# Decoder block on one core: the work between the output projection and the Strassen units in another order

## The chip, the core and the metric

One core of one Trainium2 chip runs the whole block in one launch. Its engines are TensorE (PE; its weight loads are listed as PEld), VectorE (DVE), ScalarE (ACT), GpSimd (POOL) and SyncE (SP, which only issues DMAs here); each runs its own queue in order and waits for others by semaphores. The metric is the device time of an execution in microseconds (us), lower is better. A time is the median of several executions; the profile is one execution more, with a time of its own.

## What is computed

x is 512 tokens by 1024 features in float32. After a mixer stage (gated linear attention, GLA, and sparse attention, NSA) the block ends with

```python
mixed = sigmoid(merge_gla) * (o_gla @ w_proj_gla) + sigmoid(merge_nsa) * (o_nsa @ w_proj_nsa)
x = x + rms_norm(mixed @ w_out, norm_mix_post)
h = rms_norm(x, norm_ffn_pre)
f = (silu(h @ w_ffn_gate) * (h @ w_ffn_up)) @ w_ffn_down     # 1024 -> 2816 -> 1024
x = x + rms_norm(f, norm_ffn_post)
```

and, in GLA, the gates are `log_sigmoid(a_lr @ w_alpha2 + b_alpha)`, whose running sums are taken per head.

## The kernel before

Features lie on the 128 partitions, tokens on the free axis (512 columns), so a matrix product is made of row blocks of 128 output features. Float32 accuracy comes from three products: each operand is split into a high part (a cast to fp32r on ACT) and a low part (the difference), and PE adds high by high, high by low and low by high. A low part is made in one of two ways: one subtraction on DVE, or a negated copy on ACT to which an accumulating DMA, issued by POOL, adds the source ("on_dma"). `Stream` (lines 32 to 75) loads weight tiles (128x1024, 512 KB) through SP one ahead and splits them; `st.on_dma` (line 172) names the tiles whose low part goes by DMA.

The stretch of the change goes so (lines 880 to 1233). The output projection has 8 row blocks; blocks 3 to 7 are made by token halves (`out_half(n, e)`, e = 0, 1 for tokens 0 to 255 and 256 to 511), first all first halves, then the second halves. Their squares are summed on POOL; `out_sums(e)` sums them over the partitions with matmuls by ones (`token_sums`) and takes the power -1/2 (`rsqrt_mean`: DVE, then POOL). `resid(e)` spreads that scale with matmuls (`over_partitions`, line 221, the "scale product"), and makes for each of 8 row blocks: x1 = out * scale + x (two DVE operations), h2h (ACT) and h2l (DVE). `resid_squares(e)` squares x1 on ACT and sums on POOL; `norm2(e)` makes from these the scale of the feed-forward norm, `normed(e)` the normed input on DVE.

The feed-forward layer has 22 row blocks. The first three ("plain" blocks, `NPLAIN`) work on the unnormed h2 and are scaled when evacuated (`plain_out`): blocks 0 and 1 by halves (`ffn_half(e, w, ps)`, gate and up weights of a block, 8 rows of k, 12 matmuls in all for a row of both blocks), block 2 in whole (`third`). The other 19 are made by Strassen-Winograd units (`unit(n)`, from N0 = 3 on): a 2x2 split of weights and inputs, gate and up products together in 7 products of 12 matmuls of 256 columns. The weights' sums s1, s2 (`prep_s`) and s3, s4 (`prep_t`) are made on DVE and split by `split_pair`; the inputs' forms b11, t2, t3, t1, b21, t4, b22 by `x_forms`. The products of a unit share two PSUM banks, and each has its evacuation before the next product into its bank.

The order on an engine is set when the program is built: a planner walks the instructions in the order in which they are written, and with its own cost estimates gives each engine the earliest written one that it takes to be ready. So a written order is a priority; `tc.issue_after(ins)` adds a fixed place behind an instruction of the same engine. A tile with a tag waits for the release of the tile that had its buffer. Before, the second residual's scale product stands behind row k = 2 of plain block 1's first half (`marks[2]`, line 1191).

The tail makes the last row block of the down projection by halves, too (lines 1272 to 1299): `tail_out(e)` multiplies by the scale, adds x1 and stores; for the second half every third add is on POOL.

Of the kernel before, what the change touches and what calls it, by code (L numbers as in the profile page):

```python
# [16 lines left out]
S = 512  # L17
# [74 lines left out]
def hybrid_block_kernel(ctx: ExitStack, tc: tile.TileContext, I, outT):  # L92
# [79 lines left out]
    st.on_dma = set(with_att) | {(x, n) for x in "gu" for n in range(1, NPLAIN)}  # L172
# [30 lines left out]
    def token_sums(acc, tag, blocks=range(NT)):  # L203

        ps = bank(tag)
        for i in blocks:
            for a in range(len(acc)):
                pe.matmul(ps[:, i:i + 1], acc[a][:, i * 128:(i + 1) * 128], ones[:, 0:1],  # L208
                          start=(a == 0), stop=(a == len(acc) - 1))
        return ps  # L210
# [127 lines left out]
    def gates_gla():  # L338
# [12 lines left out]
        for h in range(HG):  # L351
            pool.tensor_tensor(out=lam[:, h], in0=lows[h], in1=lam[:, h], op=OP.subtract)
# [555 lines left out]
    sq2 = quads("sq2_", 4, F32, "e")  # L908
# [57 lines left out]
    def resid(e, after=None):  # L966
        t = halves[e]
        rb = over_partitions(rs1, "tp", blocks[e], after)
        for k in range(KD):
# [6 lines left out]
            dve.scalar_tensor_tensor(out=lo, in0=y, scalar=g_fpre[:, k:k + 1], in1=hi.bitcast(F32),  # L976
                                     op0=OP.mult, op1=OP.subtract)
        return last

    def resid_squares(e):  # L980
        t = halves[e]
        for k in range(KD):
            act.activation(out=sq2[k // 2][:, k % 2, t], in_=x1[k][:, t], func=AF.Square)
            if k > 0:
                pool.tensor_tensor(out=sq2[0][:, 0, t], in0=sq2[0][:, 0, t], in1=sq2[k // 2][:, k % 2, t], op=OP.add)
# [3 lines left out]
    def norm2(e, after):  # L989
        r = slice(2 * e, 2 * e + 2)  # L990
        ps = token_sums([sq2[0][:, 0, :]], "tp", blocks[e])
        rsqrt_mean(rs2[:, r], ps[:, r], D, EPS)
        ps = over_partitions(rs2, "tp", blocks[e], after)
        act.copy(rb_x[:, halves[e]], ps[:, halves[e]])

    def ffn_half(e, w, ps):
# [3 lines left out]
        for k in range(KD):  # L1000
# [77 lines left out]
    sums = {}  # L1078

    def prep_s(n):  # L1080
        t = flat(ffn.tile([128, 2, S], F32, tag="sa", bufs=2, name="s12"))
        g, u = raws[n, "w_gate"], raws[n, "w_up"]
        dve.tensor_tensor(out=t[:, 0:512], in0=u[:, 0:512], in1=u[:, 512:1024], op=OP.add)
        dve.tensor_tensor(out=t[:, 512:1024], in0=t[:, 0:512], in1=g[:, 0:512], op=OP.subtract)
        sums[n] = t
        split_pair(n, t, ("s1", "s2"))

    def prep_t(n):
        t = flat(ffn.tile([128, 2, S], F32, tag="sa", bufs=2, name="s34"))
        g, u = raws.pop((n, "w_gate")), raws.pop((n, "w_up"))  # L1090
        dve.tensor_tensor(out=t[:, 0:512], in0=g[:, 0:512], in1=u[:, 0:512], op=OP.subtract)
        dve.tensor_tensor(out=t[:, 512:1024], in0=g[:, 512:1024], in1=sums.pop(n)[:, 512:1024], op=OP.subtract)
        split_pair(n, t, ("s3", "s4"))
# [8 lines left out]
    def x_form(name, segs):  # L1102

        his, los = [], []
        for src, hi, lo in segs:
            split(hi, lo, src)
# [3 lines left out]
        XF[name] = (his, los)  # L1110

    def x_forms():
        def at(i):
            return flat(hT[:, 2 * i:2 * i + 2, :]), flat(hTl[:, 2 * i:2 * i + 2, :])

        def bfull(t):
            return t.rearrange("p q t -> p (q t)")

        b11, b12, b21, b22 = [bfull(x) for x in (nb[0][0], nb[0][1], nb[1][0], nb[1][1])]
# [3 lines left out]
        t2 = [slot(4), slot(5)]  # L1123
        for i in range(2):
# [254 lines left out]
```

## Time and profile before

| | us |
|---|---|
| three executions: median (lowest to highest) | 920.99 (920.01 to 922.46) |
| the profiled execution: time | 921.21 |
| its span, first to last instruction | 919.4 |
| PE busy in it | 883.9 |
| DVE / ACT / POOL busy | 541.6 / 464.1 / 126.2 |
| mean granted TensorE clock | 0.987 |

The span is what the trace shows; the time has 1.8 us around it. A timeline row gives start, duration, engine, line of the kernel and operation, and in brackets how long the engine had been idle and what ended that. A granted clock of 1.00 is 2.4 GHz, 0.50 is 1.2 GHz. A row of PE is one matmul from its start to its modelled end, so rows overlap.

### The profile page before, as it was taken

To read this page: it belongs to the slowest core of one execution; us is meant where nothing else is said; L and a number is where in the kernel's file an instruction comes from. 1 tells how busy PE (TensorE), PEld (TensorE's weight loads), DVE (VectorE), ACT (ScalarE), POOL (GpSimd) and SP (SyncE) were. 2 spreads that over 40 slices of the span, in tenths; PEclk is the share of its full clock that TensorE was granted. 3 is DMA by queue.
4 is the path that set the end of the run, shared out by engine and by line. 5 is a ranking of instruction groups with operands and counts; after the bars stand their busy time and mean duration, and the time that the engine had idled before them with its cause. 6 is when DMAs were issued, how large, how long until landed. Compare 5 with 4: busy or idle time off the path is not lost. (4 is left out here: it accounts for less than half of the span.)

```text
span 919.4 us, 13174 instructions
## 1 busy us (share of the span) xinstructions
PE 883.9 (96%) x5074; PEld 762.0 (83%) x5074; DVE 541.6 (59%) x1008; ACT 464.1 (50%) x830; POOL 126.2 (14%) x156
## 2 busy tenths in 40 slices
PE   9999899999999999999999989799999999999995
PEld 8897677887788777777888977799999999788884
DVE  8214744443463998877675277986777778422224
ACT  6335324333442888887545447665665556323220
POOL 1100512010110000010001344021121110001011
PEclk9999899999999999999999999899999999999997
DMA  6232221312242254354237547397777772533312
GB/s 233 83 111 92 69 72 66 91 48 91 71 149 64 68 116 114 92 115 104 58 113 258 160 127 192 83 241 160 170 171 187 185 157 58 172 83 106 84 61 93
DMA packets 36480, 109.64 MB, mean 119 GB/s; under 512 B 4188, under 2 KB 6252, under 8 KB 36288
## 3 DMA queue, kind: packets, MB, share of 16 engines
q1 hardware_dynamic: 26944, 81.44, 28.6%
q0 software_dynamic: 8752, 26.80, 15.5%
q8 instruction: 40, 0.66, 0.3%
q10 hardware_dynamic: 720, 0.54, 0.2%
q14 instruction: 24, 0.20, 0.1%
HBM read 94.61 MB, written 4.19 MB: 107 GB/s over the span
## 5 line engine op out<-in xcount | busy, mean ns | idle before, releaser
L58 ACT CAST whi<-wraw 128x1024 fp32r<-128x1024 f32 (+3 forms) x98 | 96.1, 981 | 217.2 <-PE ps_mm L184 125.1
L64 DVE TENSOR_TENSOR wlo<-wraw,whi 128x1024 fp32r<-128x1024 f32 (+3 forms) x82 | 92.8, 1133 | 118.5 <-ACT whi L58 118.0
L183 PE MATMUL ps_mm<-hT_hi,whi 128*128 128x512 f32 x376 | 153.6, 408 | 2.2 <-DVE gq L296 2.2
L185 PE MATMUL ps_mm<-hT_hi,wlo 128*128 128x512 f32 x376 | 151.1, 402 | 1.3 <-DVE wlo L64 0.7
L184 PE MATMUL ps_mm<-hT_lo,whi 128*128 128x512 f32 x376 | 149.7, 398 | 0.0
L185 PEld LDWEIGHTS ps_mm<-hT_hi,wlo 128*128 128x128 f32 x376 | 71.4, 190 | 19.0 <-DVE wlo L64 1.5
L183 PEld LDWEIGHTS ps_mm<-hT_hi,whi 128*128 128x128 f32 x376 | 71.6, 190 | 17.8 <-ACT dd L370 2.6
L184 PEld LDWEIGHTS ps_mm<-hT_lo,whi 128*128 128x128 f32 x376 | 71.6, 190 | 14.9
L744 ACT ACTIVATE p<-p,mx 128x512 f32<-128x512 f32 (+1 forms) x64 | 35.9, 561 | 5.8 <-DVE mx L742 5.4
L201 DVE TENSOR_TENSOR pl<-ps_tp,ph 128x512 fp32r<-128x512 f32 (+1 forms) x64 | 31.0, 488 | 9.6 <-ACT ph L200 8.8
L62 POOL DMA_DIRECT2D wlo<-wraw x16 | 13.9, 867 | 164.5 <-ACT wlo L61 135.7
L1056 POOL DMA_DIRECT2D w_uu<-in_w_up x19 | 16.5, 867 | 145.4 <-ACT w_uu L1055 131.8
L934 POOL TENSOR_TENSOR acc<-acc,nsq 128x512 f32<-128x512 f32 x8 | 10.3, 1287 | 184.6 <-ACT nsq L933 184.6
L742 DVE CUSTOM_DVE_ANT_0 p<-ps_sc,causal 128x512 f32<-128x512 f32 (+1 forms) x64 | 29.9, 485 | 6.2 <-PE ps_sc L735 5.7
L200 ACT CAST ph<-ps_tp 128x512 fp32r<-128x512 f32 (+1 forms) x64 | 26.7, 416 | 5.8 <-PE ps_tp L784 4.1
L784 PE MATMUL ps_tp<-ident,p 128*128 128x128 f32 x160 | 27.7, 273 | 0.0
L784 PEld LDWEIGHTS ps_tp<-ident,p 128*128 128x128 f32 x160 | 20.5, 140 | 6.6
L183 PE MATMUL ps_mm<-gla_hi,whi 128*128 128x512 f32 x64 | 25.9, 405 | 0.0
L184 PE MATMUL ps_mm<-gla_lo,whi 128*128 128x512 f32 x64 | 25.4, 397 | 0.0
L185 PE MATMUL ps_mm<-gla_hi,wlo 128*128 128x512 f32 x64 | 25.4, 397 | 0.0
L1072 ACT CAST w_d0h<-s 128x1024 fp32r<-128x1024 f32 x13 | 13.6, 1047 | 23.3 <-PE ps_acc L1148 9.8
L1072 ACT CAST w_hl<-s 128x1024 fp32r<-128x1024 f32 x12 | 12.5, 1044 | 24.4 <-PE ps_tp L1148 8.7
(934 smaller groups left out, 2556.8 us busy)
## 6 DMA issues: line engine op xcount, KB each, us to landing
wraw<-in_w_t SPq DMA_DIRECT2D x40, 512.0 KB, 3.5
wraw<-in_w_gate SPq DMA_DIRECT2D x21, 512.0 KB, 5.3
rw<-in_w_up SPq DMA_DIRECT2D x19, 512.0 KB, 3.8
wlo<-wraw POOLq DMA_DIRECT2D x16, 512.0 KB, 4.5
wraw<-in_w_down SPq DMA_DIRECT2D x16, 512.0 KB, 3.6
wlo<-in_w_gate POOLq DMA_DIRECT2D x13, 512.0 KB, 8.4
wraw<-in_w_tok SPq DMA_DIRECT2D x12, 440.0 KB, 4.1
w_uu<-in_w_up POOLq DMA_DIRECT2D x19, 256.0 KB, 6.9
```

Of the source, the lines that this page charges most:

```text
L58: self.nc.scalar.copy(hi[:, :cols], raw[:, :cols])
L64: self.nc.vector.tensor_tensor(out=lo[:, :cols], in0=raw[:, :cols], in1=hi[:, :cols].bitcast(F32), op=OP.subtract)
L183: pe.matmul(ps[:, t], wh[:, c], xh(k)[:, t], start=(k == 0), stop=False)
L184: pe.matmul(ps[:, t], wh[:, c], xl(k)[:, t], start=False, stop=False)
L185: marks.append(pe.matmul(ps[:, t], wl[:, c], xh(k)[:, t], start=False, stop=(k == ktot - 1)))
L200: act.copy(hi, src)
L201: dve.tensor_tensor(out=lo, in0=src, in1=hi.bitcast(F32), op=OP.subtract)
L742: dve.tensor_tensor_reduce(out=o, in0=s, in1=causal[:, S - n:S], scale=-1.0, scalar=-NEG, op0=OP.add, op1=OP.min, accum_out=mx[:, i:i + 1])
L744: act.activation(out=o, in_=o, func=AF.Exp, scale=-1.0, bias=mx[:, i:i + 1], accum_out=z[:, i:i + 1])
L784: pe.transpose(tp[:, i * 128:(i + 1) * 128], p[:, OFF[i] + k * 128:OFF[i] + (k + 1) * 128], ident)
L1056: pool.dma_start(lo, src, accum_op=OP.add)
L1072: act.copy(hi, t)
```

## The change

Ten edits, some of them small:

- The first unit's raw weights are loaded early, once more, into two buffers (`early`), and its sums s1..s4 are made ahead of the output projection's row blocks. s1, s2 are split by ACT and an accumulating DMA behind the first residual's last cast; s3, s4 by ACT and DVE behind `x_forms`.
- u0, the up weights of plain block 0, joins the tiles whose low part is made by DMA. The up weights of block 2 get buffers of their own.
- Plain block 0's first half is cut: rows 0 and 1, `out_sums(1)`, rows 2 to 4, the second residual (its scale product behind row 4, in place of row 2 of block 1), rows 5 to 7.
- The norms' sums and scales are placed apart (`norm2_sums`, `norm2_scale`), the second half's sums before the last two rows of block 1.
- Forms b11 and b21, which need the first half only, go ahead of `normed(1)`; t2 is one tile of 1024 columns.
- Plain block 0 is evacuated before the first unit, 1 after it, 2 after the second unit.
- Later units' sums s1..s4 are made in one go (`prep_st`), the first one's behind the last form.
- `token_sums` takes all blocks of its first input first.
- The four subtractions in `gates_gla` move from POOL to DVE.
- Tail: the first half's scale product stands behind four rows of the second third of the sum, not behind all eight; every second add of the second half is on POOL.

```diff
-    st.on_dma = set(with_att) | {(x, n) for x in "gu" for n in range(1, NPLAIN)}
+    st.on_dma = set(with_att) | {("u", 0)} | {(x, n) for x in "gu" for n in range(1, NPLAIN)}
...
-        for i in blocks:
-            for a in range(len(acc)):
+        for a in range(len(acc)):
+            for i in blocks:
...
-            pool.tensor_tensor(out=lam[:, h], in0=lows[h], in1=lam[:, h], op=OP.subtract)
+            dve.tensor_tensor(out=lam[:, h], in0=lows[h], in1=lam[:, h], op=OP.subtract)
...
-    sq2 = quads("sq2_", 4, F32, "e")
+    early = [flat(quad("e%d" % i, F32, "early%d" % i)) for i in range(2)]
...
+    st.place["u", 2] = lambda: [flat(quad("e%d" % i, F32R, "u2_%d" % i)) for i in (2, 3)]
...
-    def split_pair(n, t, names):
+    def split_pair(n, t, names, after=None, on_dma=False):
         hi, lo = next_slot()
-        with tc.issue_after(h2_made.ins):
+        with tc.issue_after(after.ins) if after else nullcontext():
             act.copy(hi, t)
-        dve.tensor_tensor(out=lo, in0=t, in1=hi.bitcast(F32), op=OP.subtract)
+            if on_dma:
+                act.activation(out=lo, in_=t, func=AF.Copy, scale=-1.0)
+        if on_dma:
+            pool.dma_start(lo, t, accum_op=OP.add)
+        else:
+            dve.tensor_tensor(out=lo, in0=t, in1=hi.bitcast(F32), op=OP.subtract)
...
+    def prep_st(n, after=None):
         g, u = raws.pop((n, "w_gate")), raws.pop((n, "w_up"))
+        s12 = sums_s(g, u, after)
+        split_pair(n, s12, ("s1", "s2"))
+        split_pair(n, sums_t(g, u, s12), ("s3", "s4"))
...
-        x_form("b11", [(b11, *at(0))])
         dve.tensor_tensor(out=b11, in0=b12, in1=b11, op=OP.subtract)
...
-        x_form("b21", [(b21, flat(quad("e0", F32R, "x4h")), flat(quad("e1", F32R, "x4l")))])
...
+    for raw, x in zip(early, ("w_gate", "w_up")):
+        nc.sync.dma_start(raw, I[x][N0])
+    s12 = sums_s(*early)
+    s34 = sums_t(*early, s12)
     for n in BYHALF:
         out_half(n, 0)
-    for x in ("w_gate", "w_up"):
-        load(N0, x)
     out_half(3, 1)
     out_half(4, 1)
     out_sums(0)
+    for x in ("w_gate", "w_up"):
+        load(N0, x)
     out_half(5, 1)
-    resid(0)
+    on_act, on_dve = resid(0)
     for n in (6, 7):
         out_half(n, 1)
-    out_sums(1)
     resid_squares(0)
...
-    ffn_half(0, w0, first)
+    ffn_half(0, w0, first, range(0, 2))
+    out_sums(1)
+    marks = ffn_half(0, w0, first, range(2, 5))
+    resid(1, marks[-1])
+    ffn_half(0, w0, first, range(5, 8))
+    resid_squares(1)
+    split_pair(N0, s12, ("s1", "s2"), on_act, True)
...
-    marks = ffn_half(0, w1, second)
-    h2_made = resid(1, marks[2])
-    resid_squares(1)
-    marks = ffn_half(1, w0, first)
-    norm2(0, marks[5])
-    ffn_half(1, w1, second)
+    ffn_half(0, w1, second, range(0, 4))
+    norm2_sums(0)
+    ffn_half(0, w1, second, range(4, 8))
+    marks = ffn_half(1, w0, first, range(0, 2))
+    norm2_scale(0, marks[-1])
+    ffn_half(1, w0, first, range(2, 8))
...
     normed(0)
+    x_form("b11", [(b11, *at(0))])
+    ffn_half(1, w1, second, range(0, 6))
+    norm2_sums(1)
+    ffn_half(1, w1, second, range(6, 8))
...
+    marks = prod(third[0], w2, h2(h2h), h2(h2l), 0, 2, KD)
+    norm2_scale(1, marks[-1])
+    x_form("b21", [(b21, flat(quad("e0", F32R, "x4h")), flat(quad("e1", F32R, "x4l")))])
+    normed(1)
+    prod(third[0], [x[:, 256:1024] for x in w2], h2(h2h), h2(h2l), 2, 6, KD)
+    end = x_forms()
+    prep_g(N0)
+    prep_u(N0)
+    split_pair(N0, s34, ("s3", "s4"))
...
-    for n, (pg, pu) in enumerate((first, second, third)):
-        plain_out(n, pg, pu)
+    plain_out(0, *first)
...
         unit(n)
+        if n == N0:
+            plain_out(1, *second)
+        if n == N0 + 1:
+            plain_out(2, *third)
         if n + 1 < KF:
-            prep_s(n + 1)
-            prep_t(n + 1)
+            prep_st(n + 1, end)
...
-            eng = pool if e == 1 and k % 3 == 0 else dve
+            eng = pool if e == 1 and k % 2 == 0 else dve
...
-    down_half(1, (1,))
-    tail_out(0)
+    prod(psd, [x[:, 0:512] for x in wd[1]], fh, fl, 8, 4, KF, halves[1])
+    rb = over_partitions(rs3, "tp", blocks[0])
+    prod(psd, [x[:, 512:1024] for x in wd[1]], fh, fl, 12, 4, KF, halves[1])
+    tail_out(0, rb)
```

## Rows read from the trace of the kernel before

**Rows 1.** The page's line of the engines: busy time in us (share of the span), x instructions.
```profile
PE 883.9 (96%) x5074; PEld 762.0 (83%) x5074; DVE 541.6 (59%) x1008; ACT 464.1 (50%) x830; POOL 126.2 (14%) x156
```

**Rows 2.** Busy time of the engines in stretches: from:to, its length, then for PE, PEld, DVE, ACT and POOL the busy us (x instructions), the granted TensorE clock, the DMA engines' share, GB/s.
```profile
520.18:561.00 40.82, 36.20 (x291) 34.48 (x291) 31.10 (x65) 23.86 (x51) 18.93 (x23) 1.00 0.43 126
...
574.31:590.88 16.57, 11.03 (x64) 9.78 (x62) 16.03 (x24) 10.77 (x15) 0.87 (x1) 0.79 0.37 66
...
590.88:606.00 15.12, 15.12 (x126) 14.97 (x127) 13.71 (x21) 9.84 (x15) 2.59 (x3) 1.00 0.66 166
```

**Rows 3.** PE's timeline around the change: start, us, engine, line, operation, what it writes and reads, [idle time before it and what ended that]. L221 is a scale product, ps_tp at 523.00 for the first residual and at 545.25 for the second; 528.40 and 528.75 begin the last two rows of row block 7's second half, three matmuls each; L1148 is a Strassen unit.
```profile
523.00 0.61 PE L221 MATMUL ps_tp<-ident,rs 128*128 128x128 f32 x4
...
528.40 0.28 PE L183 MATMUL ps_acc<-hT_hi,whi 128*128 128x256 f32 x1
...
528.75 0.28 PE L183 MATMUL ps_acc<-hT_hi,whi 128*128 128x256 f32 x1
...
545.25 0.61 PE L221 MATMUL ps_tp<-ident,rs 128*128 128x128 f32 x4
...
579.14 0.58 PE L1148 MATMUL ps_tp<-hT_hi,w_d0h 128*128 128x256 f32 x1 [3.26 <-ACT hT_hi L200]
...
584.61 0.38 PE L1148 MATMUL ps_tp<-hT_hi,w_d1h 128*128 128x256 f32 x1
...
590.88 0.39 PE L1148 MATMUL ps_tp<-x4h,whi 128*128 128x256 f32 x1 [1.68 <-DVE us L1157]
```

**Rows 4.** DVE's timeline, 520 to 557, same columns: first sums of the first unit (L1083, L1092), the first and the second residual's first product (L973), u0's low part (L64), the second residual's last operation (L976).
```profile
523.10 0.69 DVE L1083 TENSOR_TENSOR s<-rw 128x512 f32<-128x512 f32 x1 [2.58 <-DMA rw<-in_w_up]
...
525.47 0.74 DVE L973 TENSOR_TENSOR slot<-slot,ps_tp 128x256 f32<-128x256 f32 x2
...
536.15 1.23 DVE L1092 TENSOR_TENSOR s<-rw,s 128x512 f32<-128x512 f32 x1
...
537.30 1.76 DVE L64 TENSOR_TENSOR wlo<-wraw,whi 128x1024 fp32r<-128x1024 f32 x1
...
545.89 0.42 DVE L973 TENSOR_TENSOR slot<-slot,ps_tp 128x256 f32<-128x256 f32 x1 [6.44 <-PE ps_tp L221]
...
556.25 0.70 DVE L976 SCALAR_TENSOR_TENSOR h2l<-slot,vecs,h2h 128x256 fp32r<-128x256 f32 x1 [0.18 <-ACT h2h L975]
```

**Rows 5.** ACT's and POOL's timeline: the cast of u0's high part, and the issue of an accumulating DMA, of plain block 2's gate weights, behind ACT's negated copy.
```profile
534.81 1.03 ACT L58 CAST whi<-wraw 128x1024 fp32r<-128x1024 f32 x1
...
538.33 0.90 POOL L62 DMA_DIRECT2D w_d1l<-wraw  x1 [0.35 <-ACT w_d1l L61]
```

**Rows 6.** DMA issues by line: count, KB each, median us from issue to landing. The first from the page, the second from the same list for 525 to 575.
```profile
wlo<-wraw POOLq DMA_DIRECT2D x16, 512.0 KB, 4.5
...
w_g3l<-in_w_gate POOLq DMA_DIRECT2D x1, 512.0 KB, 11.0
```

**Rows 7.** DVE's timeline from the second residual's end to the first unit's own evacuations: normed inputs (L1099), a difference among the forms (L1122), two low parts (L201), a plain evacuation (L1028), the unit's first evacuation (L1157).
```profile
556.87 3.73 DVE L1099 SCALAR_TENSOR_TENSOR nb<-slot,vecs,rb_x 128x256 f32<-128x256 f32 x8
...
571.16 3.25 DVE L1099 SCALAR_TENSOR_TENSOR nb<-slot,vecs,rb_x 128x256 f32<-128x256 f32 x8
...
574.33 1.22 DVE L1122 TENSOR_TENSOR nb<-nb,nb 128x1024 f32<-128x1024 f32 x1
...
580.33 2.35 DVE L201 TENSOR_TENSOR hT_lo<-nb,hT_hi 128x1024 fp32r<-128x1024 f32 x2
...
584.41 0.68 DVE L1028 TENSOR_TENSOR fa<-ps_sc,rb_x 128x512 f32<-128x512 f32 x1
...
590.41 0.41 DVE L1157 TENSOR_TENSOR us<-ps_tp,us 128x256 f32<-128x256 f32 x1
```

**Rows 8.** Timelines of POOL, DVE and PE in the GLA stage: the four subtractions of the gates (L352), the scans (L357), an evacuation (L296), a difference (L367), and the PE row that waited for the evacuation with the first and the last of twelve slow ones behind it.
```profile
90.60 6.87 POOL L352 TENSOR_TENSOR lam<-low,lam 128x512 f32<-128x512 f32 x4 [60.82 <-ACT lam L350]
...
91.91 4.47 DVE L357 TENSOR_TENSOR_SCAN lam<-keep,lam 128x512 f32<-128x512 f32 x2 [3.37 <-POOL lam L352]
...
98.80 0.68 DVE L296 TENSOR_TENSOR gq<-ps_mm,rb_x 128x512 f32<-128x512 f32 x1
...
102.89 1.09 DVE L367 TENSOR_TENSOR dd<-lam 128x512 f32<-128x512 f32 x1 [1.88 <-POOL gku L390]
...
104.65 2.70 DVE L357 TENSOR_TENSOR_SCAN lam<-keep,lam 128x512 f32<-128x512 f32 x2
...
99.62 0.47 PE L183 MATMUL ps_mm<-hT_hi,whi 128*128 128x512 f32 x1 [2.18 <-DVE gq L296]
...
101.66 0.63 PE L183 MATMUL ps_mm<-hT_hi,whi 128*128 128x512 f32 x1
...
106.36 0.63 PE L185 MATMUL ps_mm<-hT_hi,wlo 128*128 128x512 f32 x1
```

**Rows 9.** Timelines of DVE and PE in the tail: the first half's first products (L1287) and adds (L1289), PE's scale product of the second half, a pair of adds while POOL adds, DVE's last add.
```profile
904.52 0.75 DVE L1287 TENSOR_TENSOR y<-y,ps_tp 128x256 f32<-128x256 f32 x2 [3.23 <-PE ps_tp L221]
...
905.19 0.75 DVE L1289 TENSOR_TENSOR y<-y,x1r 128x256 f32<-128x256 f32 x2
...
908.97 1.12 PE L221 MATMUL ps_tp<-ident,rs 128*128 128x128 f32 x4 [1.02 <-POOL rs L215]
...
911.71 0.84 DVE L1289 TENSOR_TENSOR y<-y,x1r 128x256 f32<-128x256 f32 x2
...
915.05 0.72 DVE L1289 TENSOR_TENSOR y<-y,x1r 128x256 f32<-128x256 f32 x1
```

More of the change, by code (lines that the diff above doesn't have):

```diff
@@ L975, in resid @@
             last = act.activation(out=hi, in_=y, func=AF.Copy, scale=g_fpre[:, k:k + 1])
-            dve.scalar_tensor_tensor(out=lo, in0=y, scalar=g_fpre[:, k:k + 1], in1=hi.bitcast(F32),
-                                     op0=OP.mult, op1=OP.subtract)
-        return last
+            end = dve.scalar_tensor_tensor(out=lo, in0=y, scalar=g_fpre[:, k:k + 1], in1=hi.bitcast(F32),
+                                           op0=OP.mult, op1=OP.subtract)
+        return last, end
     def resid_squares(e):
@@ L982, in resid_squares, with norm2_sums, norm2_scale, ffn_half @@
         for k in range(KD):
-            act.activation(out=sq2[k // 2][:, k % 2, t], in_=x1[k][:, t], func=AF.Square)
+            sq = sq2[0][:, t] if k == 0 else sq2[1 + (k - 1) % 6 // 2][:, halves[(k - 1) % 2]]
+            act.activation(out=sq, in_=x1[k][:, t], func=AF.Square)
             if k > 0:
-                pool.tensor_tensor(out=sq2[0][:, 0, t], in0=sq2[0][:, 0, t], in1=sq2[k // 2][:, k % 2, t], op=OP.add)
+                pool.tensor_tensor(out=sq2[0][:, t], in0=sq2[0][:, t], in1=sq, op=OP.add)
     rs2 = ffn.tile([128, NT], F32, name="rs2")
-    def norm2(e, after):
+    def norm2_sums(e):
         r = slice(2 * e, 2 * e + 2)
-        ps = token_sums([sq2[0][:, 0, :]], "tp", blocks[e])
+        ps = token_sums([sq2[0]], "tp", blocks[e])
         rsqrt_mean(rs2[:, r], ps[:, r], D, EPS)
+    def norm2_scale(e, after):
         ps = over_partitions(rs2, "tp", blocks[e], after)
         act.copy(rb_x[:, halves[e]], ps[:, halves[e]])
-    def ffn_half(e, w, ps):
+    def ffn_half(e, w, ps, ks=range(KD)):
         t = halves[e]
         marks = []
-        for k in range(KD):
+        for k in ks:
             i, j = k // 2, k % 2
@@ L1105, in x_form @@
         for src, hi, lo in segs:
-            split(hi, lo, src)
+            act.copy(hi, src)
+            last = dve.tensor_tensor(out=lo, in0=src, in1=hi.bitcast(F32), op=OP.subtract)
             n = hi.shape[1] // 256
@@ L1110, in x_form, with at @@
         XF[name] = (his, los)
+        return last
+    def at(i):
+        return flat(hT[:, 2 * i:2 * i + 2, :]), flat(hTl[:, 2 * i:2 * i + 2, :])
     def x_forms():
[L1113 to L1119, printed above, removed]
         seg = (slice(0, 512), slice(512, 1024))
-        x_form("b11", [(b11, *at(0))])
         dve.tensor_tensor(out=b11, in0=b12, in1=b11, op=OP.subtract)
-        t2 = [slot(4), slot(5)]
-        for i in range(2):
-            dve.tensor_tensor(out=t2[i], in0=b22[:, seg[i]], in1=b11[:, seg[i]], op=OP.subtract)
-        hi, lo = at(1)
-        x_form("t2", [(t2[i], hi[:, seg[i]], lo[:, seg[i]]) for i in range(2)])
+        t2 = flat(ffn.tile([128, 2, S], F32, tag="sa", bufs=2, name="t2"))
+        dve.tensor_tensor(out=t2, in0=b22, in1=b11, op=OP.subtract)
+        x_form("t2", [(t2, *at(1))])
         dve.tensor_tensor(out=b12, in0=b22, in1=b12, op=OP.subtract)
```

47 lines of the change are left out of this document (20 added, 27 removed).

## The prediction

> **What bounds the kernel now.** I read the page's engine line first: TensorE (PE) is busy 96% of the span [rows 1], so a change of order can only win PE's waits, its half-clock time, and what comes after its last product. The table of stretches [rows 2] shows where these lie near the change. From the first half of row block 5 to the last plain half (520.18 to 561.0) PE is busy 36.2 of 40.8 us; in the first Strassen units 11.0 of 16.6, at a mean granted clock of 0.79; after 590.88 it waits no more (15.12 of 15.12 us). Busy time flatters, since a matmul's row (0.28 us) is longer than the distance to the next one, so I count work: 256-column matmuls start every 0.117 us (three in the 0.35 from 528.40 to 528.75, [rows 3]), 512-column ones take twice that. At 590.88 PE had issued 62 matmuls of Strassen units (counted in its timeline); had they run without a gap up to there, the units would have begun at 590.88 - 62 x 0.117 = 583.6. I call this the zero point of the units, and price the middle of the change by how far it moves.
>
> Then the timelines of PE and of VectorE (DVE) side by side. PE waits 3.3 us at 579.14 for a ScalarE (ACT) cast that follows a DVE chain, runs some two dozen matmuls at half clock (to 584.61), and waits 1.7 us at 590.88 for a DVE evacuation [rows 3]. DVE runs almost without a break from 571.16 to 591 [rows 7]. So DVE's queue sets the zero point, and the question is when DVE begins it and how much stands in it.
>
> **The middle: the second half's scale.** The first half's residual starts on DVE at 525.47, though its scale left PE at 523.6: the first sums of the first Strassen unit (three operations from 523.10) stand before it, the fourth at 536.15 and the low part of the up weights of plain block 0 ("u0", 1.76 us at 537.30) inside it [rows 3, 4]. The change makes the sums before 520, when DVE is idle (its sources are loaded once more, 2 x 512 KB, for which the hiding work is the row blocks of the output projection; were they late by x, DVE would start x late), and gives u0's low part to ACT and an accumulating DMA. The residual then starts at 523.7 and ends near 535, 4 to 5 us earlier.
>
> The second half's residual doesn't follow at once. Its scale is a PE product ordered behind plain block 0's fifth row, whose last matmul reads u0's low part. That is the added wait: behind it on PE stand the rest of the plain blocks, and DVE waits for the scale. u0's buffer is free when the last row block is done at about 529 [rows 3]; ACT casts u0 at 534.81 now [rows 5], as it is full of residual work, and I leave it there. High part to 535.9, negated copy 1.0 us more, 0.3 to the issue on GpSimd (POOL) [rows 5], landing 4.5 us after it in the median of such DMAs and 11.0 at the slowest [rows 6]: 541.7. Five matmuls and the scale product (0.6 us each) put DVE's start at 542.9 against 545.89 [rows 4], 3.0 us earlier. PE's own work hides this: 96 first-half matmuls and the sums, 11.7 us, are left at 529, so it runs dry only at about 541. DVE's start is bounded by 541.6 (a landing so early that PE's own work is the limit) and 549.4 (the slowest landing).
>
> The Trainium skill, "DMA: Bandwidth & Descriptors", section "Anatomy of one DMA — SWDGE (gpsimd) path", gives 2.0 us plus bytes over 436 GB/s, by which I estimate 3.2 us for 512 KB; the forecast would then be 1.3 us lower. The rows of this stretch say 4.5 and more, and I go by them.
>
> **The middle: DVE's queue up to the units.** The second residual takes 11.1 us as now (545.89 to 556.95) and ends at 553.9. Behind it, by the new order and with present durations [rows 7]: first half's normed inputs 3.7; low parts of two forms 2 x 1.2; second half's normed inputs 3.3 (they start at 571.16 now as their scale is late; its sums move to 2 us behind the residual); then x_forms: three differences 3 x 1.22, one more 1.2, four low parts of 1.2, and b22's two halves 1.3, together 11.0. Sum 20.4: 574.3; with two small scale operations 574.6. Now the first unit's second sums are split (1.22, as a difference of the same shape): 575.8. Then only the first plain block is evacuated (three operations like that at 584.41, 1.9 us; today eight of nine stand before the unit's own evacuation at 590.41): 577.7.
>
> PE in the same time: last plain half 1.4 us after the last residual row, 555.4; third block 11.2 and the two norm products 0.8: 567.4; then the unit's first two products (the second needs t2's low part, 568.2, no wait) until 570.2. There the new late thing is found: the third product needs the split of the second sums, now behind all of x_forms, at 575.8. PE waits 5.6 us, where it waited 3.3 before. Nothing covers it except products of the next unit, whose banks need the evacuation that comes later still. The clock: after today's 3.3 us wait the rows show 24 matmuls at half rate [rows 3], after the 1.7 us wait the stretch stays at full clock [rows 2, 3]. I take 24 again, 2.3 us. Third product until 578.4, its evacuation 578.8, fourth product from 578.9, half of the slow ones still to come (1.2): 36 matmuls are done, so the zero point is 578.9 - 36 x 0.117 + 1.2 = 575.9. Gain in the middle 583.6 - 575.9 = **7.7 us** (9.4 if the clock holds, 1.2 with the slowest landing; 16.2 if the split is slipped in earlier and PE never waits, zero point 567.4). The two other plain evacuations go behind the first and second unit: DVE is busy 13.7 of 15.1 us there today [rows 2] and they bring 3.8 us, but sums of later units have a whole unit (9.8 us) of room each; I cost them at nothing, and at up to 2 us if that room is gone.
>
> With one answer each: the norms' scale products, split sums and narrower squares issue the same counts on PE and POOL; the result's stores (8 x 256 KB on SP) come behind two more loads but are issued when their rows are ready; t2 in another buffer saves two DVE instruction starts, below 0.2 us.
>
> **GLA gates.** Four subtractions go from POOL (6.87 us) to DVE. Now the scan on DVE waits for the first and then runs 2 x 2.23 us beside POOL; later, with POOL idle for most of it, 2 x 1.35 [rows 8]. On DVE: 90.6 + 4 x 0.69 (a sum of this shape, [rows 4]) + 2 x 1.35 + a difference 1.1 + a half-width product 0.4 (half a pair of [rows 4]) = 97.6 for the evacuation of gq that PE waits for, against 98.80. The waits of PE that end at 99.62 and before 101.66 shrink by **1.2 us**; by nothing at the least, if DVE's order puts another operation first. If the shorter wait keeps the clock, 12 matmuls at 0.43 instead of 0.23 us (101.66 to 106.36) go too: 3.5. What wait is left lies between the 1.7 and 3.3 us of [rows 3]; I take 1.2.
>
> **Tail.** The first half's scale goes behind four rows instead of eight: DVE may start at 903.05 instead of 904.52 [rows 9]. It then has the first half done when the second scale comes; that is 0.2 us earlier because the ready sums go first, 909.9 for DVE's start against 910.7 now. One add more on POOL: twelve DVE operations instead of thirteen in the 5.05 us to 915.77, 0.4 less, with 0.1 to 0.2 back, as a pair of adds beside POOL takes 0.84 us and alone 0.75 [rows 9]. Gain **1.0 us** (0.5 to 1.3). The Trainium skill, "GPSIMD Engine Reference", section "1. Specifications", says GpSimd's SBUF interfaces are shared with VectorE and contended by two-input operations; that speaks against the added POOL add, and the 0.09 us of these pairs agrees with it, weakly.
>
> **Sum.** 7.7 + 1.2 + 1.0 = 9.9 us. The profiled execution took 921.21 (span 919.4 and 1.8 around it), 0.2 above the median of three runs, 920.99: 911.3, and against the median **911.1 us**.
>
> **Rivals.**
> (a) *The split is early.* The build's planner fills DVE's waits for ACT with the split and the unit's evacuations, PE doesn't wait, both clocks hold. For it: today low parts and a plain evacuation stand interleaved among the forms (584.41) [rows 7]. Against: DVE had hardly a gap to fill. 16.2 + 3.5 + 1.0 at the limit, 900.4; about 903 with a short wait.
> (b) *The DVE queue eats it.* The next unit's sums and splits (5.2 us) and the second plain evacuation (1.9) stand ahead of the first unit's evacuations. The zero point is 575.9 + 7.1 = 583.0, gain 0.6 + 2.2: 918.4. Against: the sums have a later place in the program.
> (c) *Slower: u0's low part.* Every us by which it lands after 541.7 goes one for one through scale, residual and forms. At 11.0 us after issue: 917.6. It decides from 14.4 us after issue (no change), and from 17.2 the kernel is slower by 2.8 us, 924. For it: accumulating DMAs of g2, u0, the first sums and u2 crowd together. Against: the 4.5 is a median of sixteen, the 11.0 a single case [rows 6].
>
> **How the numbers follow.** A measurement of this kernel can tell about 0.3% (2.8 us) from no change. Forecast, 907 to 917.5: 0.60. (a), 899 to 907: 0.22. (b), 917.5 to 922: 0.11, a fifth of it still below 918.2. (c): 0.07. Faster 0.60 + 0.22 + 0.02 = 0.84; same 0.09; slower 0.07. The range 903 to 918 leaves out (c), most of (b) and a third of (a), about 0.2.
>
> **What would show it.** First residual on DVE within 0.3 us of its scale; u0's negated copy, then a gap on PE or DVE up to its landing; second residual near 543; second norm's sums near 556; PE's longest wait in the middle before the third product of the first unit, released by a DVE split. Wrong would be: no wait there; a scale that still leaves PE at 545; a GLA wait as long as before.

## The result, and the profile after the change

| | before | after |
|---|---|---|
| median of four executions, us (lowest to highest) | 920.50 (919.39 to 922.46) | 910.09 (907.25 to 910.57) |
| ratio, 95% interval | | 0.9878 (0.9851 to 0.9905) |
| profiled execution: time, span | 921.21, 919.4 | 909.94, 908.2 |

The kernel became 10.4 us faster; 911.1 was forecast. The page's line of the engines, to be held against [rows 1]:

```profile
PE 880.6 (97%) x5074; PEld 759.3 (84%) x5074; DVE 537.6 (59%) x1006; ACT 465.3 (51%) x831; POOL 123.5 (14%) x155
```

The stretches that answer to [rows 2], moved by 2.2 us for the first and begun at the first Strassen unit for the other two; columns as there:

```profile
518.00:558.82 40.82, 37.35 (x298) 35.51 (x298) 26.62 (x62) 28.30 (x56) 21.08 (x27) 1.00 0.69 183
570.54:587.11 16.57, 15.03 (x120) 14.29 (x119) 16.05 (x23) 9.76 (x14) 1.30 (x2) 1.00 0.39 80
587.11:602.23 15.12, 15.12 (x128) 15.06 (x128) 14.93 (x25) 8.66 (x13) 2.17 (x3) 1.00 0.89 215
```

In the first unit's stretch PE was busy 11.0 us at a granted clock of 0.79 [rows 2]; now it is busy 15.0 of 16.6 at 1.00. So the wait and the half clock that the forecast kept there are gone.

To see where time came from I cut the span at PE rows that both kernels have: the spreading of the GLA gates (L332), the first GLA score (L400), the first residual's sums (L208 at 517), the first product of the down projection (L183 at 769), the tail's first sums (L208 at 890). PE's timeline after:

```profile
72.98 0.60 PE L332 MATMUL ps_tp<-ident,tokb 128*16 128x128 f32 x4
...
117.97 0.33 PE L400 MATMUL ps_tp<-gq,gke 128*64 128x64 f32 x2
...
517.19 0.39 PE L208 MATMUL ps_tp<-ones,acc 128*128 128x1 f32 x3
...
768.95 0.39 PE L183 MATMUL ps_mm<-hT_hi,whi 128*128 128x512 f32 x1
...
890.25 0.39 PE L208 MATMUL ps_tp<-ones,acc 128*128 128x1 f32 x3
```

Before, these rows begin at 73.45, 120.26, 519.37, 780.00 and 899.62; DVE's last add ends at 915.77 and 904.25. The differences give the stages:

| stage, us | before | after | gain | forecast |
|---|---|---|---|---|
| start, up to L332 | 73.45 | 72.98 | 0.47 | 0 |
| GLA, L332 to L400 | 46.81 | 44.99 | 1.82 | 1.2 |
| L400 to the first residual's sums | 399.11 | 399.22 | -0.11 | 0 |
| middle, up to the down projection | 260.63 | 251.76 | 8.87 | 7.7 |
| down projection, up to the tail's sums | 119.62 | 121.30 | -1.68 | 0 |
| tail, up to DVE's last end | 16.15 | 14.00 | 2.15 | 1.0 |

They add up to 11.5; the span is 11.2 shorter, as 0.3 more lies behind DVE's last add. The 1.7 us lost in the down projection can't be put down to the change: PE waits there for a low part of the down weights before (1.55 us) and after (1.76), and of these two profiles only the one after shows half clock behind it; seven of the experiments below have the same instructions in this stage and took 119.6 to 119.8 us. In the middle, PE's waits from 515 to 600 (us in total, times, longest):

```profile
PE ps_sc L1013 <- DMA wlo<-wraw: 1.2, 1, 1.2
PE ps_sc L1011 <- ACT h2h L977: 0.9, 3, 0.3
PE ps_tp L1154 <- DVE w_d1l L1083: 0.9, 1, 0.9
PE ps_tp L208 <- POOL acc L960: 0.8, 1, 0.8
PE ps_tp L221 <- POOL rs L215: 0.6, 1, 0.6
PE ps_sc L1012 <- DVE h2l L978: 0.6, 2, 0.4
PE ps_tp L1154 <- ACT us L1161: 0.3, 1, 0.3
PE ps_sc L1154 <- DVE fa L1033: 0.3, 1, 0.3
```

No wait reaches 1.7 us; together they are 5.6. PE's and DVE's timelines at the places that the prediction named (to hold against [rows 3, 4, 7]):

```profile
520.82 0.60 PE L221 MATMUL ps_tp<-ident,rs 128*128 128x128 f32 x4
...
538.94 0.38 PE L1013 MATMUL ps_sc<-h2h,wlo 128*128 128x256 f32 x1 [1.22 <-DMA wlo<-wraw]
...
540.58 0.61 PE L221 MATMUL ps_tp<-ident,rs 128*128 128x128 f32 x4
...
570.54 0.28 PE L1154 MATMUL ps_tp<-hT_hi,whi 128*128 128x256 f32 x1
...
575.19 0.38 PE L1154 MATMUL ps_tp<-hT_hi,w_d1l 128*128 128x256 f32 x1 [0.88 <-DVE w_d1l L1083]
```

```profile
521.47 0.75 DVE L975 TENSOR_TENSOR slot<-slot,ps_tp 128x256 f32<-128x256 f32 x2 [3.13 <-PE ps_tp L221]
...
541.22 0.75 DVE L975 TENSOR_TENSOR slot<-slot,ps_tp 128x256 f32<-128x256 f32 x2 [8.32 <-PE ps_tp L221]
...
561.59 3.26 DVE L1111 SCALAR_TENSOR_TENSOR nb<-slot,vecs,rb_x 128x256 f32<-128x256 f32 x8 [1.75 <-ACT rb_x L999]
...
573.92 1.22 DVE L1083 TENSOR_TENSOR w_d1l<-s,w_d1h 128x1024 fp32r<-128x1024 f32 x1
575.06 1.21 DVE L1119 TENSOR_TENSOR x5l<-nb,x5h 128x1024 fp32r<-128x1024 f32 x1
```

The first residual starts as its scale product ends (521.42), PE waits 1.2 us for u0's low part, the second residual starts at 541.22, and the split of the second sums (L1083 at 573.92) stands ahead of the low part of form t4 (x5l, L1119). Two rows were not foreseen: DVE's 1.75 us wait before normed(1) at 561.59, and the late start of the first unit, 570.54.

### The profile page after: what moved, and what is told of

Read it like the earlier page. It is cut to its first block, busy times and chain, and to the rows that moved or that the text cites. A ratio compares the mean times of both kernels' runs of the same rounds, so it can differ in the third digit from the quotient of the medians.

```text
span 908.2 us, 13172 instructions
## 1 busy us (share of the span) xinstructions
PE 880.6 (97%) x5074; PEld 759.3 (84%) x5074; DVE 537.6 (59%) x1006; ACT 465.3 (51%) x831; POOL 123.5 (14%) x155
## 5 line engine op out<-in xcount | busy, mean ns | idle before, releaser
L64 DVE TENSOR_TENSOR wlo<-wraw,whi 128x1024 fp32r<-128x1024 f32 (+3 forms) x81 | 91.0, 1124 | 120.1 <-ACT whi L58 119.9
L183 PE MATMUL ps_mm<-hT_hi,whi 128*128 128x512 f32 x376 | 152.9, 407 | 1.6 <-DVE gk L296 1.6
L183 PEld LDWEIGHTS ps_mm<-hT_hi,whi 128*128 128x128 f32 x376 | 71.2, 189 | 17.2 <-ACT el L371 2.0
L201 DVE TENSOR_TENSOR pl<-ps_tp,ph 128x512 fp32r<-128x512 f32 (+1 forms) x64 | 31.0, 488 | 9.6 <-ACT ph L200 8.8
L1077 ACT CAST w_d1h<-s 128x1024 fp32r<-128x1024 f32 x13 | 13.6, 1048 | 24.5 <-PE ps_sc L1154 6.5
L183 PE MATMUL ps_mm<-gla_hi,whi 128*128 128x512 f32 x64 | 25.9, 404 | 0.0
## 6 DMA issues: line engine op xcount, KB each, us to landing
w_uu<-in_w_up POOLq DMA_DIRECT2D x19, 256.0 KB, 6.9
```

The lines of the kernel that those rows point to most:

```text
L64: self.nc.vector.tensor_tensor(out=lo[:, :cols], in0=raw[:, :cols], in1=hi[:, :cols].bitcast(F32), op=OP.subtract)
L183: pe.matmul(ps[:, t], wh[:, c], xh(k)[:, t], start=(k == 0), stop=False)
L201: dve.tensor_tensor(out=lo, in0=src, in1=hi.bitcast(F32), op=OP.subtract)
```

## The experiments

Theory A, formed from the trace after: PE's own work now sets the middle, with 5.6 us of scattered waits left in it; what is late is u0's low part by DMA and what follows it (second scale, second residual, second norm). Its rivals were the prediction's view (DVE's queue up to the units sets the time) and, for each edit, that the part is hidden. e9 to e11 join several edits; the others differ from the changed kernel in one place (e2 in two, both in the tail). Ratios are to the kernel before, run on the same chip; its medians there are 919.5 to 921.8 us, so ratios compare better than medians. Stages are those of the table above, from each kernel's profile, which is one execution.

| kernel | median | ratio, 95% | GLA | middle | down | tail |
|---|---|---|---|---|---|---|
| changed | 910.1 | 0.9878 (0.9851 to 0.9905) | 45.0 | 251.8 | 121.3 | 14.0 |
| e1 GLA on POOL | 912.6 | 0.9912 (0.9880 to 0.9943) | 48.2 | 251.8 | 121.3 | 14.0 |
| e2 tail as before | 913.3 | 0.9918 (0.9898 to 0.9938) | 45.1 | 251.8 | 119.8 | 15.7 |
| e3 plain first | 911.1 | 0.9891 (0.9867 to 0.9915) | 46.3 | 253.9 | 119.6 | 14.0 |
| e4 u0 on DVE | 907.3 | 0.9856 (0.9837 to 0.9874) | 45.1 | 250.4 | 119.8 | 14.0 |
| e5 scale early | 914.4 | 0.9922 (0.9901 to 0.9943) | 46.3 | 256.0 | 119.8 | 14.0 |
| e6 split first | 909.7 | 0.9872 (0.9849 to 0.9895) | 44.9 | 251.5 | 119.6 | 14.4 |
| e7 power first | 908.2 | 0.9855 (0.9835 to 0.9876) | 45.1 | 251.2 | 119.8 | 14.0 |
| e8 down low | 907.3 | 0.9845 (0.9823 to 0.9867) | 45.0 | 251.9 | 117.7 | 14.0 |
| e9 scale early, casts placed | 910.1 | 0.9862 (0.9832 to 0.9891) | 45.1 | 252.0 | 119.8 | 14.1 |
| e10 e9 with e6, e7, e8 | 906.9 | 0.9842 (0.9821 to 0.9864) | 45.1 | 251.9 | 117.7 | 14.0 |
| e11 e4 with casts, e6, e7, e8 | 904.0 | 0.9805 (0.9781 to 0.9829) | 43.5 | 247.5 | 117.8 | 14.5 |
| e12 sums inside | 914.0 | 0.9917 (0.9887 to 0.9946) | 45.1 | 255.5 | 121.3 | 14.0 |

By its time alone only e11 can be told from the changed kernel; the other intervals overlap with its own. The middle repeats within 0.1 us wherever it wasn't touched (e1, e2, e8), so a shift of 0.3 us can be read there, as long as the granted clock is the same. It isn't in all profiles: in the middle the changed kernel is at full clock throughout, e4 and e12 are at half clock for 3.4 us each, e5, e9 and e10 for some 6.8 us each. The start can't be read so: L332 begins anywhere from 72.6 to 75.8 us in these executions.

**e1, GLA.**

```diff
-            dve.tensor_tensor(out=lam[:, h], in0=lows[h], ...
+            pool.tensor_tensor(out=lam[:, h], in0=lows[h], ...
```

> The changed kernel (910.1 us, span 908.2) with the four subtractions of the GLA gates back on POOL and nothing else. Theory read from the trace after (the stage brought 2.2 us: one of PE's two waits is gone and six matmuls fewer run at half clock): the out_sums of the first half start 2.2 us later than 517.19, and the time is 912.3. As the prediction sized it (1.2): 911.3. Rival, that the stage's 2.2 us are the chance of one execution's clock and not of the edit: 910.1, with out_sums at 517.2.

The stage is 3.2 us longer, with as much time at half clock (3.4 us) as in the changed kernel's profile, so the clock is not the cause. PE's timeline shows two waits with POOL's subtractions; before there was the first alone [rows 8], after only the second (1.63 us at 104.20):

```profile
100.11 0.48 PE L183 MATMUL ps_mm<-hT_hi,whi 128*128 128x512 f32 x1 [2.18 <-DVE gq L296]
...
108.61 0.47 PE L183 MATMUL ps_mm<-hT_hi,whi 128*128 128x512 f32 x1 [1.65 <-DVE gk L296]
```

DVE after the change makes the evacuation of gq at 93.62, counted from L332 4.7 us earlier than in [rows 8]:

```profile
92.48 1.21 DVE L357 TENSOR_TENSOR_SCAN lam<-keep,lam 128x512 f32<-128x512 f32 x1
93.62 0.66 DVE L296 TENSOR_TENSOR gq<-ps_mm,rb_x 128x512 f32<-128x512 f32 x1
...
98.21 3.25 DVE L357 TENSOR_TENSOR_SCAN lam<-keep,lam 128x512 f32<-128x512 f32 x2
```

A scan takes 1.21 us while POOL idles, 1.62 beside its later work, 2.23 in [rows 8]. The Trainium skill, "GPSIMD Engine Reference", section "1. Specifications", says that GpSimd shares its SBUF interfaces with VectorE; the scan agrees with that. By times alone e1 (912.6) can't be told from the changed kernel; the stage shows the gain.

**e2, tail.** The scale product again behind all eight rows, `k % 3` for `k % 2`.

> The changed kernel with the tail as it was (first half's scale product behind all eight rows, every third add on POOL). Theory from the trace after: from PE's first sums of the second half to DVE's last add takes 1.9 us longer than the changed kernel's, 912.0. As the prediction sized it (1.0): 911.1. Rival, that the sums' order alone brings the gain: 910.3 at most, since that order is kept here.

The tail takes 1.67 us more, of the 2.15; the other 0.48 stays with the order of the sums. The median moved more (3.2 us); for the profiled execution that is its start, 2.8 us late, for the other three no trace tells it.

**e3, plain evacuations.**

```diff
-    plain_out(0, *first)
+    for n, (pg, pu) in enumerate((first, second, third)):
+        plain_out(n, pg, pu)
...
-        if n == N0:
-            plain_out(1, *second)
-        if n == N0 + 1:
-            plain_out(2, *third)
```

> The changed kernel with all three plain blocks evacuated before the first unit's own evacuation, as before the change. Theory A (after the change PE's own work sets the start of the units, and DVE has only 1 us to spare in the first unit): the unit's evacuation waits for four to six more DVE operations of 0.65 us, PE waits 2 to 3 us more, 912 to 914. Theory of the prediction (DVE's queue sets the units' zero point, the deferral is worth its 3.8 us): 913.9, and PE's longest wait there is over 3 us. Rival: DVE makes it up within the two units, 910.1.

The middle is 2.1 us longer. PE's waits grow little (0.6 us for ACT's cast of the next unit's weights and 0.5 for a unit's evacuation are new): less than the 3.8 us of DVE work that went ahead. By the stage the size is near the lower end of Theory A (2 to 3 us), by its time (911.1) e3 lies below A's 912; the prediction's 3.8 us does not come, nor does the rival's nothing.

**e4, u0's low part.** `("u", 0)` out of `st.on_dma`.

> The changed kernel with the low part of plain block 0's up weights made by one DVE subtraction again. Theory A (the landing of the accumulating DMA at 538.9 now sets the second residual's scale, and DVE idles 8 us before it): the low part is ready by about 534, PE's wait of 1.2 us is gone, the scale leaves PE 1 to 2 us earlier, 908.5 to 909.5. Theory of the prediction (DVE's work before the second residual counts): the first residual ends 1.2 to 1.8 us later and the time is 911 to 912. Rival: neither is on the path, 910.1.

The middle is 1.3 us shorter, the median lower, though the intervals overlap. DVE's timeline: the subtraction inside the first residual, then the second residual's first product:

```profile
531.91 1.78 DVE L64 TENSOR_TENSOR wlo<-wraw,whi 128x1024 fp32r<-128x1024 f32 x1
...
536.28 0.75 DVE L975 TENSOR_TENSOR slot<-slot,ps_tp 128x256 f32<-128x256 f32 x2 [0.83 <-PE ps_tp L221]
```

Counted from the first sums (518.06 here, 517.19 in the changed kernel) the second residual starts at 18.2 us instead of 24.0. So this edit of the change costs time: the DMA's landing, not DVE's 1.8 us, was in the chain. The 1.3 us are a lower bound, since behind a wait of 1.2 us this profile has a stretch at half clock (columns as in [rows 2]), where some 16 matmuls start 0.21 us apart instead of 0.12, about 1.5 us in all:

```profile
550.40:553.80 3.40, 3.40 (x18) 3.40 (x17) 2.41 (x5) 3.40 (x4) 0.42 (x1) 0.50 1.01 349
```

**e12, first sums.** The four sums inside the first residual again, their sources still loaded early.

> The changed kernel with the four sums of the first unit not ahead of the row blocks but inside the first residual, behind its first product (4 x 0.69 us on DVE); their sources are still loaded early. Theory A (u0's negated copy on ACT stands behind the first residual's casts, so its DMA, the second scale and the residual behind it follow the first residual one for one): PE's wait for u0's low part grows from 1.2 to about 4 us, the stretch from the first sums to the down product takes 253.8 to 254.6 instead of 251.8 us, the time is 912 to 913. Theory of the prediction (u0's cast keeps its place whatever the first residual does) and rival (DVE idles 8 us before the second residual and covers it): 251.8 us, 910.1.

The middle is 3.7 us longer, more than A said. ACT's negated copy of u0 (L61), and PE's wait for its landing:

```profile
537.11 1.04 ACT L61 ACTIVATE wlo<-wraw 128x1024 fp32r<-128x1024 f32 x1
...
543.36 0.39 PE L1016 MATMUL ps_sc<-h2h,wlo 128*128 128x256 f32 x1 [2.09 <-DMA wlo<-wraw]
```

From the first sums (519.49) the copy begins 17.6 us, in the changed kernel (532.25 less 517.19) 15.1 us later; PE's wait for u0 ends at 23.9 instead of 21.8 us. That is 2.1 of the 3.7; the rest fits the clock, 0.85 from 540 to 547, where the changed kernel shows 1.00. So the early sums pay some 2 us, but through ACT's queue and u0's DMA.

**e5 and e9, the scale.** e5 takes the scale product out from behind u0's low part; e9 also holds back ACT's casts of the next units' weights.

```diff
-            marks.append(last)
+                marks.append(last)        # a mark for each weight's row
...
-    resid(1, marks[-1])
+    resid(1, marks[0])        # third gate row of block 0
```
```diff
     def dma_split(hi, lo, raw, src, cast=None):
-        act.copy(hi, raw)
+        with tc.issue_after(cast.ins) if cast else nullcontext():
+            act.copy(hi, raw)
...
+    prep_g(N0 + 1, cast=scale_copy)           # prep_u alike
...
+            prep_g(n + 2, cast=casts["t2"] if n == N0 else None)
```

> The changed kernel with the second residual's scale product ordered behind the gate weights' third row of plain block 0, so that it doesn't stand behind any product with u0's low part. Theory A (u0's landing sets the second residual, and through it PE's waits up to the units): the scale leaves PE near 532 instead of 540.6, DVE begins the residual near 533 instead of 541.2, and PE's waits behind it (h2h 0.9, h2l 0.6, the second norm 0.6, the second sums' split 0.9 us) go: 907 to 908; PE's wait for u0 itself stays. Rival B (ACT is full from 528.8 to 538, and the residual's casts delay u0's negated copy): PE's wait for u0 grows by what the others lose, 910 to 911. Rival C (PE's own work covers all): 910.1.

> The kernel with the second residual's scale product behind the third gate row (its run: 914.4 us), and besides ACT's casts of the next two units' gate weights, and of the next unit's up weights, placed behind the second norm's scale copy and behind the form t2. From the first half's sums on PE to the first down product the changed kernel needs 251.8 us, the one with the early scale 256.0. Theory A (there ACT stood 9.2 us behind the load of a later unit's weights, and PE's 6.4 us wait for a form's cast is its consequence; the early scale itself is good): that wait is gone, the stretch takes 247 to 249.5 us, the time is 905.5 to 908. Rival B (the early scale itself costs, ACT being full, whatever is cast next): 254 to 256, 913 or more. Rival C (PE's own work covers the earlier scale): 251.8, 910.

In e5 the scale product starts at 532.13, and PE does begin the units earlier: 49.1 us after the first sums in e5, e9 and e10 (567.36 less 518.26 in e5), 53.4 in the changed kernel. And yet e5 is slower by 4.2 us in the middle, outside all its forecasts. Its timelines of POOL (issues of block 2's accumulating DMAs), SP (loads of later units), ACT and PE:

```profile
546.89 0.87 POOL L62 DMA_DIRECT2D w_d1l<-wraw  x1
548.97 0.86 POOL L62 DMA_DIRECT2D u<-wraw  x1 [1.20 <-ACT u L61]
...
553.18 2.80 SPq L1055 DMA_DIRECT2D wraw<-in_w_gate  x2
...
560.71 1.05 ACT L1059 CAST whi<-wraw 128x1024 fp32r<-128x1024 f32 x1 [9.19 <-DMA wraw<-in_w_gate]
...
575.29 0.58 PE L1154 MATMUL ps_tp<-hT_hi,w_d1h 128*128 128x256 f32 x1 [6.37 <-ACT hT_hi L1118]
```

The residual's casts push ACT's copies for block 2 back, so POOL issues their DMAs at 546.89 and 548.97 (536.44 and 538.33 in the changed kernel). These hold the raw buffers: the first lands at 553.13, the loads begin at 553.18. ACT, in order, stands 9.2 us at a cast of a later unit's weights, and the forms' casts stand behind it, until PE waits 6.4 us. With the casts placed (e9) ACT still stands at the next load,

```profile
565.90 0.62 ACT L1060 CAST w_uu<-rw 128x512 fp32r<-128x512 f32 x1 [4.49 <-DMA rw<-in_w_up]
```

and PE waits 2.6 and 0.8 us; behind the first wait it is at half clock, where some 26 matmuls start 0.21 us apart instead of 0.12, about 2.5 us in all:

```profile
573.00:579.90 6.90, 6.11 (x27) 5.81 (x28) 6.90 (x9) 4.00 (x5) 0.86 (x1) 0.51 0.46 78
```

The middle is back at 252.0, which is rival C's number, but not for its reason: PE had begun the units 4.2 us earlier and lost that again. By that estimate it would be near 249.5 without the half clock, the edge of Theory A. So the early scale brings PE forward, and what takes it back is ACT, which is pushed back by the residual's casts and then stands at late loads, with the clock on top. The runs don't part these, and whether an early scale pays with all loads in time wasn't tried.

**e6, e7, e8, single waits.** e6 writes the second sums' split behind form t3, e7 puts the power ahead of POOL's DMA issue, e8 asks for the down weights' second tile before the low parts of f17 to f21:

```diff
         split(hi, lo, fr[k])
         FH[k], FL[k] = hi, lo
+        if k == 16:
+            sd.ahead_to(2)
```

> The changed kernel with the split of the first unit's second sums written behind the form t3 instead of behind all forms. Theory A (the third product's wait of 0.88 us for that split is what is late there): the wait is gone and the time is 909.2. Rival: the forms that are pushed back are needed as soon, and the wait only changes its name: 910.1.

> The changed kernel with POOL's issue of the first unit's gate DMA placed behind the power of the second norm's scale, where it now stands ahead of it. Theory A (that issue makes the power 1.81 instead of 1.15 us long and later by 0.7, and DVE's wait of 1.75 us before normed(1) is its consequence): normed(1) starts 1 to 1.5 us earlier than 561.59, PE's 0.62 us wait for the power goes and the 0.88 us wait for the split shrinks: 908.8 to 909.5. Rival: the a11 product then waits for the DMA's landing instead, or the time doesn't move since other waits take its place: 910.1 or more.

> The changed kernel with the first down weights' second tile asked for before the low parts of f17 to f21 are made, so that DVE makes its low part five operations earlier. Theory A: PE's wait of 1.76 us at 776.92 is gone, and with it the eight matmuls at half clock behind it (0.43 instead of 0.23 us, 1.6 us): 906.7. If only the wait goes: 908.3. Rival: the low part of f17 or the next tile is then late by as much: 910.1.

e6 brings 0.3 of 0.9 us: its wait goes, others of 0.4 and 0.3 come. e7 brings 0.6; the power is short again, but the split's wait grows to 1.1. In the changed kernel POOL shows the long power beside the issue:

```profile
557.94 0.90 POOL L1061 DMA_DIRECT2D wlo<-in_w_gate  x1 [3.19 <-ACT wlo L1060]
558.57 1.81 POOL L215 TENSOR_TENSOR rs<-rs,mhalf 128x2 f32<-128x2 f32 x1
```

e8 brings 2.0 us of the down stage against 119.8, and 3.6 against the changed kernel's profile, where the wait was followed by half clock:

```profile
776.92 0.50 PE L185 MATMUL ps_mm<-f8p,wlo 128*128 128x512 f32 x1 [1.76 <-DVE wlo L64]
...
778.01 0.63 PE L183 MATMUL ps_mm<-f10p,whi 128*128 128x512 f32 x1
```

**e10, e11, together.**

> The kernel with the early scale and the placed casts, and besides the power ahead of the gate DMA's issue, the second sums' split behind t3, and the down weights' second tile asked for early. If the gains stand beside each other (0.35 and 0.6 us in the stretch from the first sums to the down product, 2.0 us of the down wait, on the early scale's 247 to 249.5): 902 to 905. Rival: the pow and the split wait are covered by the earlier residual, only the down wait's 2.0 us adds: 903.5 to 906.

> The changed kernel with u0's low part on DVE (its run: 907.3 us), the power first, the second sums' split behind t3, the placed casts and the down weights' second tile early; the scale's place as in the changed kernel. If the gains add: 907.3 less 0.9 less 2.0, 904.4. Rival: with u0 on DVE the residual is already where the other two would put it, and only the down wait adds: 905.3.

e10 gets only e8's gain: its middle is 251.9, as e9's, again with a wait for a form's cast (3.2 us) and half clock behind it. e11 beats both kernels: 904.0 us, ratio 0.9805. Its middle is 247.5, 3.0 shorter than e4's, where e6 and e7 alone promised 0.9. Some 1.5 us of that is e4's half clock, which e11 doesn't have; for the rest, with the residual early and the casts placed no wait in it reaches 1 us. The placed casts weren't tried on e4 alone. PE's waits from 513 to 598:

```profile
PE ps_tp L208 <- POOL acc L960: 0.8, 1, 0.8
PE ps_sc L1011 <- ACT h2h L977: 0.6, 1, 0.6
PE ps_sc L1012 <- DVE h2l L978: 0.5, 2, 0.3
PE ps_sc L1159 <- DVE fa L1033: 0.4, 1, 0.4
PE ps_tp L1159 <- DVE us L1168: 0.4, 1, 0.4
PE ps_tp L1159 <- DVE wk L1172: 0.3, 1, 0.3
```

## Why the prediction came out right, step by step

**The sum** was right by terms that erred both ways: start 0.5, GLA 1.8 for 1.2, middle 8.9 for 7.7, tail 2.15 for 1.0, and 1.7 us given back in a stage that it had left out, by a half clock that it couldn't know. That the sum met the median within 1 us is in good part luck.

**Middle, the second scale.** Right, with one part late and one early. The middle begins 2.2 us earlier in the changed kernel; with these added (the axis of before) u0's low part lands at 541.1 (541.7 forecast) and the second residual starts at 543.4 (542.9 forecast), with 13 matmuls instead of five between the landing and the scale product. "I leave it there", of ACT's cast of u0, was wrong: the copy moved forward with the residual (e12), while the DMA landed 4.6 us after its issue as in [rows 6]. The three accumulating DMAs behind it took 6.2, 8.3 and 10.4 us, at a DMA share of 1.04 from 537 to 555. The estimate of 3.2 us from the Trainium skill, "DMA: Bandwidth & Descriptors", section "Anatomy of one DMA — SWDGE (gpsimd) path", is below all four; the rows decide. That the DMA, as against DVE's subtraction, puts a landing into the chain was foreseen as the added wait, but not that DVE's subtraction would have been 1.3 us cheaper or more (e4). The place of the scale product itself, on which the 7.7 us rest, was put back in no run: of the 8.9 us the runs show some 2 for the early sums (e12), 2.1 for the deferral (e3) and a loss of 1.3 or more for u0's DMA (e4); the rest is read from rows.

**Middle, PE's work.** The step that failed is "last plain half 1.4 us after the last residual row, 555.4". 1.4 us is that row's own 12 matmuls at 0.117, as if PE had nothing else left. Already before, PE began its last plain matmul 4.0 us after the second residual's end (556.95, [rows 4]); after the change it is 4.2 us (554.14 to 558.36), and the residual took 12.9 us instead of 11.1, with three of the first half's normed inputs (L1111) among its rows. The rows, PE before, DVE and PE after:

```profile
560.98 0.28 PE L1008 MATMUL ps_mm<-h2h,w_uu 128*128 128x256 f32 x1
...
553.67 0.47 DVE L978 SCALAR_TENSOR_TENSOR h2l<-slot,vecs,h2h 128x256 fp32r<-128x256 f32 x1
...
558.36 0.28 PE L1013 MATMUL ps_mm<-h2h,w_uu 128*128 128x256 f32 x1
```

On the axis of before that half ended at 560.5 and the first unit began at 572.7, 5.3 late. PE had its own queue: the second halves' 96 matmuls, 11.2 us at 0.117, began at 542.90 and took 15.5 us, with 1.5 us of waits and with sums, a scale product and the third block's first products among them. The forecast's 567.4 is 48.0 us after the first sums; no run came below 49.1, not even those whose scale product comes 9.5 us earlier, counted from there (e5, e9, e10).

So PE came to the third product 5.3 us later, the split only 1.5 (577.3 on that axis, 575.8 forecast), also because the planner slipped it ahead of t4's low part, as rival (a) had it. The wait shrank to 0.9 of the 5.6 us forecast, and the half clock that it would have brought (2.3 us) didn't come. The two errors, 5.3 us one way and 4.7 and 2.3 the other, all but cancelled: the middle's number is right by luck. That PE's work is near the bound fits e3 (3.8 us of DVE work ahead cost 2.1), e4 (a second residual 5.8 us earlier brought 1.3, about 2.8 without its half clock) and e6. So PE's own work sets most of the units' start, and a chain through u0's DMA still costs on top of it (e4, e12).

**Middle, deferral.** "I cost them at nothing" is right for what they delay: PE is busy 15.12 of 15.12 us behind 587.11. That they bring 3.8 us is wrong, 2.1.

**GLA.** Right in kind, small in size: the wait for gq went altogether, as the planner put one scan and the evacuation first, and a wait of 1.6 us for gk took its place. With POOL's subtractions the second wait comes as well (e1); in the profile of before the slow matmuls behind the first wait hid it, as far as the rows tell. So the 1.8 us compare two single executions; with POOL's subtractions in the changed kernel the difference is 3.2 (e1).

**Tail.** Right in kind, 2.15 for 1.0. From the tail's first sums, DVE begins the second half 9.63 us later (899.88), before 11.1, of which the sums' order is 0.48 (e2) where 0.2 was put; and the second half takes 4.4 us on DVE, before 5.05. One add of 0.4 us went to POOL, and DVE's last add takes 0.50 us instead of 0.72 [rows 9]. In e6 and e11, with the same instructions in the tail, it took 14.4 and 14.5 us instead of 14.0, so the gain is 1.7 to 2.15. DVE's timeline, second half and last add:

```profile
899.88 1.08 DVE L1311 TENSOR_TENSOR y<-y,ps_tp 128x256 f32<-128x256 f32 x3 [0.25 <-PE ps_tp L221]
...
903.75 0.50 DVE L1313 TENSOR_TENSOR y<-y,x1r 128x256 f32<-128x256 f32 x1
```

**Rivals.** (a) came true in part, without its time, since PE was late itself. (b) and (c) did not come; (c)'s mechanism is real (e12: PE's wait for u0 ended 2.1 us later, and the middle took 3.7 us more, part of it at half clock). Of the signs named, the gap up to u0's landing came and the third product did wait for a DVE split; but PE's longest wait was the 1.2 us for u0.

## What to carry to other kernels

When a wait is removed, follow two clocks: when the data are ready, and when the engine is through with what it already has; the later one counts. How far the engine runs behind stands in the old trace: 4.0 us here, where 1.4 was put. Before a stage's length is given a cause, look at its granted clock; here it moved single stages by 1.3 to 2.5 us. A low part given to a DMA frees an engine but puts issue and landing into the chain and keeps the source buffer: on a stretch where that chain sets the end, 1.8 us of an engine that idles 8 us afterwards is cheaper. On an in-order engine, look for the operation that waits for a load: all that is behind it pays.

## What the runs showed of the hardware

- The same wait of 1.6 to 1.8 us at the start of the down projection was followed by half clock in the profiles of the changed kernel, e1 and e12 (121.3 us), and by full clock in those of e2 to e7 and e9 (119.6 to 119.8): 1.5 us that differ between executions of the same instructions.
- In GLA alike: behind the waits that e3 and the changed kernel have in common, the stage took 46.3 and 45.0 us; e11, with no slow matmul there, 43.5.
- A two-column power on POOL took 1.81 us beside a DMA issue, 0.71 in e7, where the issue comes behind it, and 0.71 to 0.88 in the middle of e5, where it stands alone.
